# A modulation tile that feeds four column groups, a generator stopped before its last step, and a weight split in two instructions

## The chip, the cores and the metric

The kernel runs on one core of a Trainium2 chip. Its time is the device time of one execution in microseconds (us), the median of the runs taken. Engines are named as in the profile: PE multiplies matrices (PEld is its weight load), DVE, ACT and POOL are the vector, scalar and GpSimd engines, SP issues most of the DMAs. "L577" is line 577 of the kernel.

## The reference

Two layers of a diffusion-style backbone work on 512 latent tokens and 256 context tokens, 1024 wide. Each layer takes six modulation vectors (shift, scale and gate, twice) from a small matrix product of a conditioning vector, normalises and modulates the tokens, mixes them, and runs a gated feed-forward net with a three-tap convolution. The change touches the modulation and the mixer of layer 0:

```python
mod_l = (silu_c @ ada_w[l] + ada_b[l])[:, None, :]        # 1024 x 6144 weights, per layer
mod_c = (silu_cc @ ada_w[l] + ada_b[l])[None, None, :]
sh1, sc1, g1, sh2, sc2, g2 = jnp.split(mod_l, 6, axis=-1)

def even_mixer(hl, hc, w_in, lb, onorm_w, vnorm_w, ws, bs, w_out, with_ctx):
    pl = hl @ w_in                                        # 1024 x 3584 weights
    ...
    al, ac = hgrn2_mixer(...)                             # four heads of a gated linear recurrence
    yl = jnp.concatenate([al, chunk_mlp(...)], -1) @ w_out   # chunk_mlp: gelu(u) * (ws @ norm(gelu(v)))
```

The mixer of layer 1 is a multi-head attention with a Fourier branch beside it; it is not edited, but the modulation of layer 1 is computed while it runs.

## The kernel before, in words

Every large matrix product is done with three fp32r products: a weight and an activation are each split into a high and a low part, and `mm3` (L508 to L510) multiplies high by high, high by low and low by high. A weight chunk is loaded into `raw` by SP (L329), cast to its high part `wh` by ACT (L486), and the low part `wl` is raw minus high, for most chunks one POOL instruction of 128x1024 (L498). A chunk's `raw` comes free for the next load when both have read it.

**Modulation.** `ada_group` computes a third of a layer's modulation. Its weights come in 16 tiles of 128x1024, two for each of eight steps k. The left operand `sc_pad` has only 32 columns (two of them real), so a matmul uses one of four groups of 32 columns of the array and writes 32 partitions of one PSUM bank. A tile makes two matmuls of 512 columns (L577), into the column groups 0 and 1 for an even tile, 2 and 3 for an odd one. Group 1 of layer 0 to group 0 of layer 1 run beside the mixer's input projections (`tick` advances them), the other two groups of layer 1 beside the first steps of the attention: their tiles are loaded into `kt` buffers and later into `ada_t` buffers. The very first part of layer 0's modulation (`first_mods`, L709) already uses all four column groups from one tile, with matmuls of 128 columns.

**Mixer of layer 0.** For each of four heads, four projections (`proj`, L508 to L510) run on PE, and the recurrence of the head before, a generator `gla`, is advanced in steps between them. Its inner steps go round PE (L827, L855), DVE (L848, L868, L870, L872) and ACT (L835). Its end normalises the head's output on DVE (a Newton iteration for the reciprocal root, L460 to L465, then L930), turns it on PE (L939), and splits it (L943, L944). After the last head come the projections `ev_vp` of the gated MLP, whose norm is applied by six POOL instructions (L997), `drain("gla")` (L998), and then four gate projections.

**Order.** The code is written in one order, and a scheduler puts each engine's instructions in another, by its own estimate of when they will be ready; only the first 70 us are placed by hand. So where a line stands in the code doesn't say where it stands on its engine.

Of the kernel before, what the change touches and what calls it, by code (L numbers as in the profile page):

```python
# [16 lines left out]
ALU = mybir.AluOpType  # L17
# [3 lines left out]
P = 128  # L21
D = 1024
KD = D // P
# [263 lines left out]
class _Stream:  # L287
# [112 lines left out]
    def next(self, key):  # L400
        assert self.items[self.pos] == key, (self.items[self.pos], key)
        if self.pos:
            k = self.items[self.pos - 1]
            self.live.pop(k)
            self.own -= set(k[2:])
        while key not in self.hl:
            self.prep()
        while self.ready():
            self.prep()
        self.pos += 1  # L410
        self.load(2 if self.part is None else 3)
        return self.hl.pop(key)
# [3 lines left out]
def backbone(ctx: ExitStack, tc, w, xt, ada, vec, cst, msk, rop, wst, bs, pew, out):  # L416
    nc = tc.nc
    V, S, G, T = nc.vector, nc.scalar, nc.gpsimd, nc.tensor
# [25 lines left out]
    def vcol(name, j=0, n=1):  # L444
        o, wd = VEC[name]
        return vt[:, o + j:o + j + n]

    mods = [cp.tile([P, 48, 2], F32, name=f"mods{l}") for l in range(2)]
# [3 lines left out]
    sc_pad = cp.tile([P, KD, 32], F32, name="sc_pad")  # L452
# [31 lines left out]

    def split(kind, raw, h, l):
        S.copy(h, raw)  # L486
        if kind[:5] == "down1":
            n = raw.shape[-1] // 2
            for e, c in ((G, slice(0, n)), (V, slice(n, 2 * n))):
                e.tensor_tensor(l[:, c], raw[:, c], h[:, c].bitcast(F32), op=ALU.subtract)  # L490
            return
        if kind in by_half:
            for c in range(2):
                c = slice(c * raw.shape[-1] // 2, (c + 1) * raw.shape[-1] // 2)
                G.tensor_tensor(l[:, c], raw[:, c], h[:, c].bitcast(F32), op=ALU.subtract)  # L495
            return
        e = G if kind in on_pool else V
        e.tensor_tensor(l, raw, h.bitcast(F32), op=ALU.subtract)  # L498

    by_half = {"qb_a", "kvb_k", "kvb_v", "od_out"}  # L500
    on_pool = {"dft_c", "ev_v", "qb_a", "qb_b", "kvb_k", "kvb_v", "od_out", "ev_out", "dft_t", "down0_3", "od_f", "od_q", "od_kv", "ev_in", "ev_vp", "up0", "up1"}
# [11 lines left out]
    bg = {"gla": deque(), "ada": deque(), "sum": deque()}  # L513
# [11 lines left out]
    def drain(kind):  # L525
        while advance(kind):
            pass
# [39 lines left out]
    def ada_group(l, g, rest, by=1):  # L567
        base = (l * 3 + g) * 16
        ps = bank("ad")
        for k in range(KD):  # L570
            for hf in range(2):
                i = base + 2 * k + hf
                ada_load(i + 1)
                t = ada_raw.pop(i)
                for j in range(2):
                    q = 2 * hf + j
                    T.matmul(ps[32 * q:32 * q + 32, :], sc_pad[:, k, :], t[:, j * 512:(j + 1) * 512],  # L577
                             start=(k == 0), stop=(k == KD - 1))
            if k % by < by - 1:
                continue  # L580
            ada_load(min(base + 2 * k + 4 + by, 64 if base < 64 else 96))
            for _ in range(rest):
                yield
        asb = tp.tile([P, 512], F32, tag="t2k", name="asb")
        S.copy(asb[:], ps[:])
        yield
        pt = bank("ad")
        for b in range(4):
            T.transpose(pt[:, b * P:(b + 1) * P], asb[:, b * P:(b + 1) * P], ident)
        o = mods[l][:, g * 16:(g + 1) * 16, :].rearrange("p (j b) c -> p b j c", b=4)  # L590
        i0 = pt[:].rearrange("p (b j r) -> p b j r", b=4, r=32)[:, :, :, 0:2]
        i1 = vcol("ada_b", l * 48 + g * 16, 16).rearrange("p (j b) -> p b j", b=4).unsqueeze(3)
        for b in range(4):
            V.tensor_tensor(o[:, b], i0[:, b], i1[:, b].to_broadcast([P, 4, 2]), op=ALU.add)
        yield


# [142 lines left out]
    with tc.manual_schedule(engines={ET.PE, ET.Activation, ET.DVE}):  # L740
# [16 lines left out]
        for s in (1, 0):  # L757
            a, n = SEGS[s]
# [9 lines left out]
        for kk in range(4):  # L768
            wh, wl = ws.next(("ev_v", kk))
            for j in range(2):  # L770
                k = 2 * kk + j
# [23 lines left out]
    def proj(key, src):  # L795

        wh, wl = ws.next(key)
        ps = (bank("mm"), bank("mm"))
        for k in range(KD):
            a = (wh[:, k * P:(k + 1) * P], wl[:, k * P:(k + 1) * P])  # L800
            for s in range(2):
                mm3(ps[s][:, 0:SEGS[s][1]], a, sl(src[k], s), k == 0, k == KD - 1)
            tick()
        return ps

    def gla(h, QG, FF, Y):
        q, sg = QG[:, 0, :], QG[:, 1, :]
# [33 lines left out]
        for lv in range(7):  # L841
# [3 lines left out]
            if lv < 5:  # L845
                dims = [[2 * m, 16 // m], [NT + m, 2], [1, m]]
                ps = blocks(lambda a: pick(QQ, a, dims))
                V.copy_predicated(near[:], mk[:, 32 * lv:32 * lv + 32].unsqueeze(1).to_broadcast([P, 6, 32]), ps)  # L848
            else:
                dims = [[2 * m, P // (2 * m)], [NT + m, 2], [1, m]]  # L850
                for s, (a0, n) in enumerate(SEGS):
                    ps = bank("sc")
# [30 lines left out]
        for g0 in range(0, 10, 4):  # L883
            grp = items[g0:g0 + 4]
            ps = bank("st")
# [5 lines left out]
        for g0 in range(0, 10, 4):  # L891
            grp = items[g0:g0 + 4]
            ps = bank("st")
            for j, (d, i, c) in enumerate(grp):
                T.matmul(ps[:, j * P:(j + 1) * P], KT[:, (g0 + j) * P:(g0 + j + 1) * P], vtile(c, h),
                         start=True, stop=True)
            for j, (d, i, c) in enumerate(grp):
                e = g0 + j
# [10 lines left out]
        for s, (a0, n) in enumerate(SEGS):  # L909
            ps = bank("sc")  # L910
            for j in range(n // P):
                c = a0 // P + j
                o = ps[:, j * P:(j + 1) * P]
                more = [(d, seqs[d].index(c)) for d in range(2) if seqs[d].index(c) > 0]
                T.matmul(o, SC[:, 0, c * P:(c + 1) * P], vtile(c, h), start=True, stop=not more)
                for x, (d, i) in enumerate(more):
                    e = d * 5 + i - 1
                    T.matmul(o, QQ[:, 1 - d, c * P:(c + 1) * P], st[:, e * P:(e + 1) * P],
                             start=False, stop=x == len(more) - 1)
            for j in range(n // P):  # L920
                c = a0 // P + j
# [6 lines left out]
        for s, (a0, n) in enumerate(SEGS):  # L928
# [1 line left out]
            V.tensor_tensor(SC[:, 1, a0:a0 + n].rearrange("p (c t) -> p c t", c=nj),  # L930
                            po[s][:, 0:n].rearrange("p (c t) -> p c t", c=nj),
                            rr[:, a0 // P:a0 // P + nj].unsqueeze(2).to_broadcast([P, nj, P]), op=ALU.mult)
        yield
        Y[h] = xslot()
        for s, (a0, n) in enumerate(SEGS):
            ps = bank("sc")
            for j in range(n // P):
                c = a0 + j * P
# [11 lines left out]
    for h in range(NH_A):  # L950
        QG = xslot(F32)
        FF = xslot(F32)
        for part in (0, 2, 3, 4):
            ps = proj(("ev_in", part * 4 + h), X)
# [40 lines left out]
    for c in range(6):  # L995
        a = vp[c // 3][:, c % 3, :].rearrange("p (g d) -> p g d", g=4)
        G.tensor_tensor(a, a, mr[:, c * 4:c * 4 + 4].unsqueeze(2).to_broadcast([P, 4, P]), op=ALU.mult)  # L997
    drain("gla")  # L998
    for g in range(4):
        ps = proj(("ev_in", 20 + g), X)  # L1000
        U = xcp.tile([P, 2, NT], F32, tag="xc", name="U")
        Y[4 + g] = xslot()
        for s, (a0, n) in enumerate(SEGS):
            u = U[:, 0, a0:a0 + n]
            S.activation(u, ps[s][:, 0:n], AF.Gelu_apprx_tanh)
        for s, (a0, n) in enumerate(SEGS):
            nj = n // P
            p2 = bank("sc")
            for j in range(nj):
                c = a0 // P + j  # L1010
                T.matmul(p2[:, j * P:(j + 1) * P], vp[c // 3][:, c % 3, g * P:(g + 1) * P],
                         wstt[:, g * P:(g + 1) * P], start=True, stop=True)
            z = U[:, 1, a0:a0 + n]
            V.scalar_tensor_tensor(z.rearrange("p (c t) -> p c t", c=nj),
                                   p2[:, 0:n].rearrange("p (c t) -> p c t", c=nj), vcol("vnorm", g),
                                   bsb[:, g * P:(g + 1) * P].unsqueeze(1).to_broadcast([P, nj, P]),
                                   op0=ALU.mult, op1=ALU.add)
            V.tensor_tensor(z, z, U[:, 0, a0:a0 + n], op=ALU.mult)
            yh, yl = sl(Y[4 + g], s)
            S.copy(yh, z)  # L1020
            G.tensor_tensor(yl, z, yh.bitcast(F32), op=ALU.subtract)
# [858 lines left out]
```

## Time and profile before

| | |
|---|---|
| median of 3 runs | 1649.61 us (1648.12 to 1650.98) |
| profiled execution, its own time | 1649.35 us |
| its span, first to last instruction | 1647.6 us |
| PE busy | 1591.9 us (97%) |
| DVE, ACT, POOL busy | 1140.8, 703.4, 649.1 us |
| mean granted clock of PE | 0.992 |

The profile is one execution. In its rows an fp32 matmul shows as two records, so "x4" of L577 are two matmuls. A row of a timeline or of the chain of waits has a start and a length in us; a run of equal instructions is merged into one row with its count. "[0.64 <-DVE qk L868]" behind a row is idle time of the engine just before it, and what ended that.

### The profile page before, as it was taken

The numbers are of one execution on the slowest core, as the hardware profiler recorded it, in microseconds if no ns is written. First come the engines' busy times: TensorE is split into PE (matmuls) and PEld (weight loads), VectorE is DVE, ScalarE is ACT, GpSimd is POOL, SyncE is SP. The second block draws the span as 40 slices with busy tenths as digits, with TensorE's granted clock in tenths as the row PEclk, the third lists the DMA queues.
The fourth block names the chain that finished last, engine by engine and source line by source line (L and its number), as shares of the span: only waits on it lengthen the run. The fifth ranks groups of instructions, "written<-read, shape, count | busy, mean of one in ns | idle before, by whom it ended". The sixth has DMA issues, their size and how long they took to land.

```text
span 1647.6 us, 28314 instructions
## 1 busy us (share of the span) xinstructions
PE 1591.9 (97%) x11206; PEld 1420.5 (86%) x11206; DVE 1140.8 (69%) x2134; ACT 703.4 (43%) x1328; POOL 649.1 (39%) x421
## 2 busy tenths in 40 slices
PE   8999999989999999999999999898899899999998
PEld 7777777678989999999999989676799898999997
DVE  5447675753565666676666775767874799999984
ACT  4323333523444333233332444465665555555551
POOL 1221223344625566565665513331208322323321
PEclk9999999999999999999999999999999999999999
DMA  9453434333412121222212322752105223223222
GB/s 355 159 187 116 142 116 137 120 102 103 130 50 64 61 80 55 74 77 62 80 55 75 90 68 82 250 171 93 52 27 167 90 85 108 103 90 116 103 78 77
DMA packets 53205, 175.11 MB, mean 106 GB/s; under 512 B 5712, under 2 KB 7760, under 8 KB 53072
## 3 DMA queue, kind: packets, MB, share of 16 engines
q1 hardware_dynamic: 51632, 170.66, 31.1%
q10 hardware_dynamic: 1440, 2.64, 0.4%
q8 instruction: 88, 1.44, 0.3%
q14 instruction: 45, 0.37, 0.1%
HBM read 171.18 MB, written 2.10 MB: 105 GB/s over the span
## 4 chain that ended last, share of the span: by engine, by line
PE 79%; DVE 14%; ACT 2%; DMA 2%; issue 2%; POOL 1%; DVEq 0%; SPq 0%; ACTq 0%; POOLq 0%
PE mm L508 17%; PE mm L510 16%; PE mm L509 16%; PE aux L508 7%; PE aux L509 7%; PE aux L510 7%; PE aux L577 2%; DVE qk L870 1%; DVE qk L868 1%; DVE wp L387 1%; PE aux L1143 1%; PE mm L1730 1%; DMA x<-in_xt_dram 1%; DMA raw<-in_w_dram 1%; PE aux L1749 1%
## 5 line engine op out<-in xcount | busy, mean ns | idle before, releaser
L498 POOL TENSOR_TENSOR wl<-raw,wh 128x1024 fp32r<-128x1024 f32 (+5 forms) x100 | 210.2, 2104 | 356.6 <-ACT wh L486 304.5
L486 ACT CAST wh<-raw 128x1024 fp32r<-128x1024 f32 (+5 forms) x155 | 146.5, 947 | 141.0 <-PE mm L509 63.8
L387 POOL TENSOR_TENSOR wp<-sum,wp 128x512 fp32r<-128x512 f32 x80 | 115.9, 1454 | 163.4 <-ACT wp L385 153.9
L508 PE MATMUL mm<-xt,wh 128*128 128x256 f32 (+1 forms) x384 | 135.1, 353 | 0.9 <-ACT xt L648 0.9
L510 PE MATMUL mm<-xt,wl 128*128 128x512 f32 (+1 forms) x384 | 129.4, 338 | 0.0
L509 PE MATMUL mm<-xt,wh 128*128 128x512 f32 (+1 forms) x384 | 129.3, 337 | 0.0
L509 PE MATMUL mm<-slot,wh 128*128 128x512 f32 (+1 forms) x336 | 113.4, 338 | 1.0 <-POOL slot L1253 0.7
L508 PE MATMUL mm<-slot,wh 128*128 128x512 f32 (+1 forms) x336 | 113.5, 339 | 1.0 <-ACT slot L1252 1.0
L510 PE MATMUL mm<-slot,wl 128*128 128x512 f32 (+1 forms) x336 | 113.1, 337 | 0.0
L385 ACT CAST wp<-sum 128x512 fp32r<-128x512 f32 x100 | 60.8, 620 | 122.2 <-PE aux L509 61.5
L1028 DVE SCALAR_TENSOR_TENSOR xl<-mm,mods,xl 128x512 f32<-128x512 f32 (+1 forms) x84 | 58.5, 696 | 70.7 <-PE mm L510 70.2
L495 POOL TENSOR_TENSOR wl<-raw,wh 128x512 fp32r<-128x512 f32 (+2 forms) x50 | 55.7, 1135 | 129.1 <-ACT wh L486 123.6
L387 POOL TENSOR_TENSOR wp<-raw,wp 128x512 fp32r<-128x512 f32 x60 | 80.0, 1341 | 52.3 <-ACT wp L385 52.3
L385 ACT CAST wp<-raw 128x512 fp32r<-128x512 f32 x100 | 62.1, 621 | 78.5 <-DMA raw<-in_w_dram 27.7
L508 PEld LDWEIGHTS mm<-xt,wh 128*128 128x128 f32 x384 | 72.0, 188 | 27.0 <-issue 16.8
L508 PE MATMUL mm<-kt,wp 128*128 128x256 f32 x320 | 90.4, 282 | 3.8 <-ACT t L1216 3.8
L490 POOL TENSOR_TENSOR wl<-raw,wh 128x512 fp32r<-128x512 f32 x22 | 35.7, 1622 | 138.0 <-DVE t L1245 92.3
L510 PE MATMUL mm<-kt,wp 128*128 128x256 f32 x320 | 89.8, 281 | 0.0
L509 PE MATMUL mm<-kt,wp 128*128 128x256 f32 x320 | 89.7, 280 | 0.0
L510 PEld LDWEIGHTS mm<-xt,wl 128*128 128x128 f32 x384 | 72.3, 188 | 8.2
L509 PEld LDWEIGHTS mm<-xt,wh 128*128 128x128 f32 x384 | 72.2, 188 | 8.3
L509 PE MATMUL mm<-lt,wh 128*128 128x256 f32 (+2 forms) x236 | 78.1, 331 | 1.2 <-DVE lt L1253 1.2
(390 smaller groups left out, 5272.7 us busy)
## 6 DMA issues: line engine op xcount, KB each, us to landing
raw<-in_w_dram SPq DMA_DIRECT2D x162, 512.0 KB, 3.5
ada_t<-in_ada_dram SPq DMA_DIRECT2D x80, 512.0 KB, 4.4
raw<-in_w_dram SPq DMA_DIRECT2D x31, 384.0 KB, 3.1
wp<-in_w_dram SPq DMA_DIRECT2D x20, 512.0 KB, 4.4
kt<-in_ada_dram SPq DMA_DIRECT2D x16, 512.0 KB, 7.0
raw<-in_w_dram SPq DMA_DIRECT2D x10, 256.0 KB, 2.6
xl<-in_xt_dram SPq DMA_DIRECT2D x2, 1024.0 KB, 8.0
out_dram<-xl SPq DMA_DIRECT2D x8, 256.0 KB, 2.0
```

What stands on the lines that cost most here:

```text
L385: S.copy(h, a)
L387: e.tensor_tensor(l, a, h.bitcast(F32), op=ALU.subtract)
L486: S.copy(h, raw)
L490: e.tensor_tensor(l[:, c], raw[:, c], h[:, c].bitcast(F32), op=ALU.subtract)
L495: G.tensor_tensor(l[:, c], raw[:, c], h[:, c].bitcast(F32), op=ALU.subtract)
L498: e.tensor_tensor(l, raw, h.bitcast(F32), op=ALU.subtract)
L508: T.matmul(ps, a[0], b[0], start=first, stop=False, **kw)
L509: T.matmul(ps, a[0], b[1], start=False, stop=False, **kw)
L510: T.matmul(ps, a[1], b[0], start=False, stop=last, **kw)
L577: T.matmul(ps[32 * q:32 * q + 32, :], sc_pad[:, k, :], t[:, j * 512:(j + 1) * 512], start=(k == 0), stop=(k == KD - 1))
L868: V.tensor_tensor(qa, qa, pick(FF[:], NT + m, [[2 * m, nb], [-(NT + m), 2], [0, m]]), op=ALU.mult)
L1028: V.scalar_tensor_tensor(xs, ps, gate, xs, op0=ALU.mult, op1=ALU.add)
```

## The change

Three edits. A modulation tile is now used in four matmuls of 256 columns, one for each column group, and the even tile fills the left half of the bank, the odd tile the right half; the bias addition that reads the turned result is re-indexed. The generator `gla` stops before its last step under the name "tail", the mixer runs it that far instead of to its end, and drains it after the first gate projection. And the low part of a mixer weight (`ev_v`, `ev_in`, `ev_vp`, `ev_out`) is computed by two POOL instructions, one for each half of the chunk's columns.

```diff
     def split(kind, raw, h, l):
         S.copy(h, raw)
-        if kind[:5] == "down1":
+        if kind[:5] == "down1" or kind[:3] == "ev_" and kind in on_pool:
             n = raw.shape[-1] // 2
-            for e, c in ((G, slice(0, n)), (V, slice(n, 2 * n))):
+            for e, c in ((G, slice(0, n)), (V if kind[:2] == "do" else G, slice(n, 2 * n))):
                 e.tensor_tensor(l[:, c], raw[:, c], h[:, c].bitcast(F32), op=ALU.subtract)
             return
...
                 t = ada_raw.pop(i)
-                for j in range(2):
-                    q = 2 * hf + j
-                    T.matmul(ps[32 * q:32 * q + 32, :], sc_pad[:, k, :], t[:, j * 512:(j + 1) * 512],
-                             start=(k == 0), stop=(k == KD - 1))
+                for q in range(4):
+                    T.matmul(ps[32 * q:32 * q + 32, hf * 256:(hf + 1) * 256], sc_pad[:, k, :],
+                             t[:, q * 256:(q + 1) * 256], start=k + hf == 0, stop=k + hf == KD, skip_group_check=True)
...
-        yield
+        yield "tail"
         Y[h] = xslot()
...
-    drain("gla")
+    while next(bg["gla"][0]) != "tail":
+        pass
     for g in range(4):
         ps = proj(("ev_in", 20 + g), X)
+        drain("gla")
```

On PE, in the first steps of the attention, this is what stands around the first two `kt` tiles that are used alone. Before (`kt` is a modulation tile, `lt` the latent query, `wh` and `wl` its weight, `mm` and `aux` PSUM banks):

```order
L508 MATMUL mm_10147<-wh_10022,lt_9912 128x384 [waits Activation_49]
L509 MATMUL mm_10147<-wl_10023,lt_9912 128x384 [waits Pool_49]
L577 MATMUL aux_10080<-kt_10089,sc_pad_88 32x512 [waits DMAHW5_49]
L577 MATMUL aux_10080<-kt_10089,sc_pad_88 32x512
L510 MATMUL mm_10147<-wh_10022,lt_9912 128x384 [waits DVE_49]
L508 MATMUL mm_10147<-wh_10135,lt_9913 128x384 [waits Activation_49]
L509 MATMUL mm_10147<-wl_10136,lt_9913 128x384 [waits Pool_49]
L510 MATMUL mm_10147<-wh_10135,lt_9913 128x384 [waits DVE_49]
L577 MATMUL aux_10080<-kt_10091,sc_pad_88 32x512 [waits DMAHW6_49]
L577 MATMUL aux_10080<-kt_10091,sc_pad_88 32x512
```

And after:

```order
L508 MATMUL mm_10307<-wh_10166,lt_10056 128x384 [waits Activation_49]
L576 MATMUL aux_10224<-kt_10241,sc_pad_88 32x256 [waits DMAHW5_49]
L576 MATMUL aux_10224<-kt_10241,sc_pad_88 32x256 x3
L509 MATMUL mm_10307<-wl_10167,lt_10056 128x384 [waits Pool_49]
L510 MATMUL mm_10307<-wh_10166,lt_10056 128x384 [waits DVE_49]
L508 MATMUL mm_10307<-wh_10295,lt_10057 128x384 [waits Activation_49]
L509 MATMUL mm_10307<-wl_10296,lt_10057 128x384 [waits Pool_49]
L510 MATMUL mm_10324<-wh_10166,lt_10055 128x384
L510 MATMUL mm_10307<-wh_10295,lt_10057 128x384 [waits DVE_49]
L576 MATMUL aux_10224<-kt_10243,sc_pad_88 32x256 [waits DMAHW6_49]
L576 MATMUL aux_10224<-kt_10243,sc_pad_88 32x256 x3
```

Each of the two tiles stands alone between the same projections in both programs, one or two matmuls earlier or later; two matmuls of 512 columns have become four of 256.

On PE at the last head's turning (L939), in the first gate projection (`xt` the activations, `scr` the head's output). Before:

```order
L508 MATMUL mm_3465<-xt_550,wh_3319 128x512
L509 MATMUL mm_3465<-xt_550,wh_3319 128x512
L939 MATMUL aux_3445<-ct_74,scr_748 128x128 [waits DVE_49]
L939 MATMUL aux_3445<-ct_74,scr_748 128x128 x3
L939 MATMUL aux_3453<-ct_74,scr_748 128x128 [waits DVE_49,Activation_49]
L939 MATMUL aux_3453<-ct_74,scr_748 128x128
L589 MATMUL aux_3487<-ct_74,asb_3473 128x128 x4
L510 MATMUL mm_3465<-xt_550,wl_3320 128x512
```

And after:

```order
L508 MATMUL mm_3576<-xt_553,wh_3443 128x512
L509 MATMUL mm_3576<-xt_553,wh_3443 128x512
L939 MATMUL aux_3585<-ct_74,scr_753 128x128 [waits DVE_49]
L939 MATMUL aux_3585<-ct_74,scr_753 128x128 x3
L939 MATMUL aux_3593<-ct_74,scr_753 128x128 [waits DVE_49,Activation_49]
L939 MATMUL aux_3593<-ct_74,scr_753 128x128
L588 MATMUL aux_3613<-ct_74,asb_3599 128x128 x4
L510 MATMUL mm_3576<-xt_553,wl_3444 128x512 [waits Pool_49]
```

Nothing moved here but the wait of the last row, which is for the second half of the weight's low part.

## Rows read from the trace of the kernel before

**Rows 1.** The page's table of engines: busy us, share of the span, instructions.

```profile
PE 1591.9 (97%) x11206; PEld 1420.5 (86%) x11206; DVE 1140.8 (69%) x2134; ACT 703.4 (43%) x1328; POOL 649.1 (39%) x421
```

**Rows 2.** The page's chain that ended last: share of the span by engine.

```profile
PE 79%; DVE 14%; ACT 2%; DMA 2%; issue 2%; POOL 1%; DVEq 0%; SPq 0%; ACTq 0%; POOLq 0%
```

**Rows 3.** The timeline of PE where two modulation tiles are used one right behind the other (four matmuls), and the projection behind them.

```profile
70.18 1.06 PE L577 MATMUL aux<-ada_t,sc_pad 128*32 128x512 f32 x8
71.17 0.50 PE L508 MATMUL mm<-xt,wh 128*128 128x512 f32 x1
```

**Rows 4.** The timeline of PE where `first_mods` uses two tiles, sixteen matmuls of 128 columns, four in each column group, and the projection behind them.

```profile
29.18 1.08 PE L709 MATMUL aux<-ada_t,sc_pad 128*32 128x128 f32 x32
30.20 0.50 PE L508 MATMUL aux<-wh,xt 128*128 128x512 f32 x1
```

**Rows 5.** The chain of waits from 1052 to 1076.5 us, in order of time: of its pieces on L577 the first and the last of the six with one tile that come before the one with three tiles (x12), that one, and one more with one tile.

```profile
1053.03 0.98 PE aux L577 x4
...
1067.54 0.98 PE aux L577 x4
1072.92 1.84 PE aux L577 x12
...
1075.24 0.98 PE aux L577 x4
```

**Rows 6.** The timeline of PE where one matmul of a modulation tile stands alone (two records), and what follows.

```profile
208.66 1.05 PE L577 MATMUL aux<-ada_t,sc_pad 128*32 128x512 f32 x2
209.63 0.49 PE L918 MATMUL aux<-qk 128*128 128x128 f32 x2
```

**Rows 7.** The chain of waits from 1086 to 1176 us: pieces on L577 that hold fewer than two whole tiles or are split, and a load on the chain.

```profile
1124.91 1.01 PE aux L577 x4
...
1128.01 3.42 DMA ada_t<-in_ada_dram
...
1131.48 1.05 PE aux L577 x4
...
1134.59 1.43 PE aux L577 x6
...
1136.61 0.98 PE aux L577 x2
```

**Rows 8.** The waits of PE over the whole span: what it waited for, us in total, times, the longest.

```profile
PE aux L827 <- DVE qk L868: 5.2, 4, 1.6
PE aux L939 <- DVE scr L930: 5.2, 2, 5.0
...
PE aux L827 <- ACT scr L835: 2.2, 1, 2.2
...
PE aux L855 <- DVE qk L868: 1.2, 2, 0.6
...
PE mm L510 <- DVE xt L733: 0.6, 1, 0.6
```

**Rows 9.** Groups of POOL instructions by form: busy us, mean ns, idle before.

```profile
L498 POOL TENSOR_TENSOR wl<-raw,wh 128x1024 fp32r<-128x1024 f32 x56 | 135.3, 2416 | 290.2 <-ACT wh L486 273.0 <-PE aux L855 14.3 <-PE aux L827 2.8
...
L944 POOL TENSOR_TENSOR slot<-slot 128x512 fp32r<-128x512 f32 x4 | 5.2, 1296 | 4.4 <-ACT slot L943 4.4
```

**Rows 10.** The timelines of POOL and of DVE in the last head's normalisation.

```profile
337.10 6.03 POOL L997 TENSOR_TENSOR vp<-vp,mr 128x512 f32<-128x512 f32 x6 [2.50 <-DVE mr L465]
...
337.01 0.17 DVE L926 TENSOR_SCALAR ss<-ss 128x6 f32<-128x6 f32 x1
337.21 0.95 DVE L460 TENSOR_SCALAR rr<-ss 128x6 int32<-128x6 int32 x1
...
342.18 0.96 DVE L463 TENSOR_TENSOR rst<-ss,rr 128x6 f32<-128x6 f32 x1
343.18 0.17 DVE L464 SCALAR_TENSOR_TENSOR rst<-rst,rr 128x6 f32<-128x6 f32 x1
```

**Rows 11.** The timelines of POOL and DVE at one low part of a mixer weight, and the same DVE line with POOL idle.

```profile
307.56 2.41 POOL L498 TENSOR_TENSOR wl<-raw,wh 128x1024 fp32r<-128x1024 f32 x1 [7.40 <-ACT wh L486]
...
307.66 3.12 DVE L868 TENSOR_TENSOR qk<-qk,slot 128x768 f32<-128x768 f32 x1
...
314.71 0.95 DVE L868 TENSOR_TENSOR qk<-qk,slot 128x768 f32<-128x768 f32 x1
```

**Rows 12.** The timelines of POOL and DVE at two low parts, one right behind the other.

```profile
59.64 5.22 POOL L498 TENSOR_TENSOR wl<-raw,wh 128x1024 fp32r<-128x1024 f32 x2 [7.93 <-ACT wh L486]
...
59.33 3.29 DVE L729 SCALAR_TENSOR_TENSOR mt<-x,w,rall 128x256 f32<-128x256 f32 x2
62.55 3.26 DVE L733 SCALAR_TENSOR_TENSOR xt<-mt,mods,xt 128x256 fp32r<-128x256 f32 x2
```

**Rows 13.** Busy us (and instructions) of PE, PEld, DVE, ACT and POOL in three stretches, with the clock that PE was granted, the DMAs' share and GB/s.

```profile
340.00:344.28 4.28, 0.00 (x0) 0.00 (x0) 3.97 (x10) 0.00 (x0) 3.12 (x4) 1.00 0.76 283
344.28:347.69 3.41, 2.77 (x12) 2.67 (x13) 2.39 (x8) 0.83 (x2) 0.13 (x1) 0.50 0.00 1
1080.00:1190.00 110.00, 98.19 (x638) 78.75 (x636) 90.87 (x274) 67.03 (x169) 26.94 (x26) 0.98 0.30 104
```

More of the change, by code (lines that the diff above doesn't have):

```diff
@@ L589, in ada_group @@
             T.transpose(pt[:, b * P:(b + 1) * P], asb[:, b * P:(b + 1) * P], ident)
-        o = mods[l][:, g * 16:(g + 1) * 16, :].rearrange("p (j b) c -> p b j c", b=4)
+        o = mods[l][:, g * 16:(g + 1) * 16, :].rearrange("p (f j e) c -> p f e j c", f=2, e=2)
         i0 = pt[:].rearrange("p (b j r) -> p b j r", b=4, r=32)[:, :, :, 0:2]
-        i1 = vcol("ada_b", l * 48 + g * 16, 16).rearrange("p (j b) -> p b j", b=4).unsqueeze(3)
+        i1 = vcol("ada_b", l * 48 + g * 16, 16).rearrange("p (f j e) -> p f e j", f=2, e=2).unsqueeze(4)
         for b in range(4):
-            V.tensor_tensor(o[:, b], i0[:, b], i1[:, b].to_broadcast([P, 4, 2]), op=ALU.add)
+            f, e = divmod(b, 2)
+            V.tensor_tensor(o[:, f, e], i0[:, b], i1[:, f, e].to_broadcast([P, 4, 2]), op=ALU.add)
         yield
```

## The prediction

> **What bounds the kernel now.** I read the engine table first, then the chain that ended last, then the waits of PE, and only then the timelines of the places that the diff touches. PE is busy for 97% of the span [rows 1] and holds 79% of the chain, DVE 14% [rows 2]. So PE work taken away counts where it lies on the chain, and a DVE or POOL instruction counts where a wait of PE ends on it; the waits of PE are few, and the ones that this change can reach are listed in [rows 8]. No wait of PE ends on a weight's high or low part (`wh`, `wl`), so the weights themselves are early everywhere. The sum is made against the profiled execution, 1649.35 us, 0.26 below the median of the three runs.
>
> **Edit 1: a tile feeds four column groups.** In layer 0 the two tiles of a step mostly stand right behind each other, and PE already runs their four matmuls beside each other in four column groups: from their start to the next matmul 0.99 us pass [rows 3]. A tile that stands alone has two matmuls in two groups, and takes 0.98 us on the chain [rows 5]: half the work in the same time, since each group still streams 2 records of 512 columns. What counts is the columns that the fullest group streams: 1024 in both cases; 2048 where three tiles stand together, 1.84 us [rows 5]. That gives (1.84 - 0.98) / 1024 = 0.84 ns a column and 0.12 us around it.
>
> With the change one tile puts 2 records of 256 columns into each group: 512 columns, so 0.12 + 0.43 = 0.55, and 0.43 us less. I take 0.41, since `first_mods` shows four groups fed from one tile with many short records: eight records of 128 columns in each group, again 1024 columns, take 1.02 us where two of 512 take 0.99 [rows 4, 3], so six more records cost 0.03. That row is also the proof that four groups can read one tile at once.
>
> - Attention's first steps, 1052 to 1076 us: seven tiles alone and one group of three lie on the chain [rows 5], and the order keeps all eight where they were. Gain 7 x 0.41 + 0.43 = 3.3 us. PE is what holds this stretch up; the tiles come in about as they are used, so part may turn into waiting for a load. Lower bound half of it, 1.6.
> - Later attention, 1086 to 1176: two tiles alone, 1.01 and 1.05, and a knot of 1.43 + 0.98 [rows 7], which becomes 1 + 7 + 1 matmuls, about 0.55 + 1.00 + 0.55. That would be 0.41 + 0.41 + 0.31 = 1.1 us, but a load of 3.42 us stands on the chain ahead of the second [rows 7], and in 1080 to 1190 DVE is busy for 91 and PE for 98 of 110 us [rows 13], each waiting for the other. I take 0.4, bounds 0 and 1.1.
> - Layer 0: one matmul of a tile alone costs 0.97 us [rows 6] and becomes 0.55: 0.4. A second one of this kind ends in a wait for DVE, so nothing. Bounds 0 and 0.8.
> - About 30 places where the tiles stand in pairs get two more records in each group, 0.01 us each: 0.3 us slower.
>
> The Trainium skill speaks against this edit: "TensorEngine Tiling (Array Packing)", Instruction Overhead, gives each matmul about 60 cycles, whatever its size. By that page the 160 further matmuls, 320 records, at 25 ns (60 cycles of the 2.4 GHz clock, an estimate) would cost 8 us and eat the whole gain. The trace disagrees here: 24 more records than in a pair of tiles cost 0.03 us [rows 3, 4], since those of different groups start beside each other.
>
> **Edit 2: the last head's output is turned later.** PE waits 5.0 us for L930 ahead of L939 [rows 8], and the half-rate clock of the 3.41 us behind it (0.50 granted [rows 13]) costs 1.7 more. But the order of PE shows L939 on the same place in both programs, behind the same matmul of the first gate projection, and DVE's order around L930 is the same too: the scheduler had already laid the projection over the drain. So nothing is saved. What causes this wait stays: six POOL instructions L997 run for 6.03 us from 337.10, and in that time each small DVE instruction takes 0.95 where it takes 0.17 before and behind [rows 10].
>
> **Edit 3: the low part in two halves.** One low part takes POOL 2.42 us [rows 9]; for a half I take the 128x512 subtraction of L944, 1.30 us [rows 9]. Two make 2.6, so 48 chunks cost POOL 48 x 0.15 = 7 us more; it is busy 39% [rows 1], and PE never waits for `wl`, so that and the earlier first half are worth nothing. SP's loads of `raw` wait for POOL and come 0.15 later; two of them also stand behind a pair of modulation loads that they stood ahead of. The weights are early enough for both.
>
> What does count is DVE. L868 takes 0.95 us with POOL idle and 3.12 when it starts just behind a low part [rows 11]: it stands until POOL's instruction ends, as L460 to L463 stand behind L997 [rows 10]. And where POOL has a next instruction ready, the waiting DVE instruction still gets in between: in [rows 10] one per POOL instruction, and in [rows 12] two low parts take 5.22 us, not 2 x 2.42, since a DVE instruction held the second up. So with halves a standing instruction is let in after 1.30 us instead of 2.42, and gains 1.1. If a second one of the kind follows, it stands behind the second half: 1.30 + 1.30 + about 0.4 of holding up + 0.8 = 3.8 us, against 2.42 + 0.8 + 0.95 = 4.2 before. So 1.1 us where one instruction matters, 0.35 where two do.
>
> The waits of PE that end on such a DVE instruction: L827 and L855 on L868 (5.2 and 1.2), on L835, which follows L870 (2.2), and L510 on L733 (0.6) [rows 8]. Eight waits, 9.2 us. L733's 0.6 goes whole. Of the L855 waits the first, 0.6, is [rows 11], with nothing behind it: whole. Of the others I count four at 0.35, two at nothing: 1.4. Together 2.6 us. Bounds: 1.1 for each as far as the wait is that long, 6.7; and, if the second half is let in ahead of DVE each time, 8 x 0.15 = 1.2 slower. At the tail a small DVE instruction ahead of L997 stands 0.15 longer: 0.15 slower.
>
> The Trainium skill has this as a rule ("SBUF — State Buffer", Who interferes with whom): a DVE instruction with two SBUF inputs and a GpSimd one that reads SBUF exclude each other, and the one that was issued first has it for its whole length. The trace agrees: 3.12 against 0.95 [rows 11]. By that rule two halves are two holds, which is what the 0.35 and 1.1 above rest on.
>
> **The sum.** -3.3 - 0.4 - 0.4 + 0.3 - 2.6 + 0.15 = -6.25 us: 1643.1 for the profiled execution, 1643.3 against the median. All bounds on the good side: -3.3 - 1.1 - 0.8 + 0.3 - 6.7 = -11.6, 1638; all on the bad side: -1.6 + 0.3 + 1.2 + 0.15 = +0.05, 1649.7.
>
> **The rivals.**
>
> - A, the tiles' gain is swallowed: loads or DVE set the pace of the attention's first steps, and PE waits where it worked. For it: the load on the chain in [rows 7], and DVE's 91 of 110 us in [rows 13]. Against it: seven of the eight groups of [rows 5] are chain pieces with PE work before and behind. Then 2.6 + 0.4 - 0.45 = 2.5 remain: 1647.1.
> - B, the halves give nothing: POOL's second half is let in ahead of the waiting DVE instruction. Against it stand [rows 10, 12]. Then -4.1 + 0.3 + 1.2 + 0.15: 1647.1.
> - C, slower: the modulation's matmuls have new lengths, and the scheduler has put the attention's steps between 1080 and 1190 us in another order on PE, DVE and ACT. PE is idle there for 110 - 98.19 = 11.8 us [rows 13]. If that order makes a reduction or a turn late, waits grow; it decides once they grow by more than the 6.25 gained. At double the idle time: 1649.6 - 6.25 + 11.8 = 1655.2. For it: no rule makes the new order better or worse; against it: its moves are by a few places each, and none crosses a projection.
> - D, edit 2 works after all, because DVE reaches L930 earlier: 5.0 + 1.7 us more, 1636.6. Against it: the unchanged order and L997.
> - E, four groups cannot read one tile side by side and run in turn: a tile takes 4 x 0.43 + 0.12 = 1.84 us, so each of 30 pairs 3.6 for 1.0 and each of 9 lone tiles 1.84 for 0.98, 78 + 8 us in all: near 1735. Against it: [rows 4].
>
> **How the numbers follow.** Forecast (edits 1 and 3 as priced, the new order neutral within 2 us) 0.60; A 0.13; B 0.11; C 0.09; D 0.05; E 0.02. A difference of 0.2%, 3.3 us, is about what a measurement of this kernel can tell from none. The forecast lies under 1646.3 with nine parts in ten, and D with it: faster 0.54 + 0.05, and a third of A and B, where the bounds give more than the price: 0.67. Slower: C, E, and a little of the bad bounds: 0.11. The rest, 0.22, is no change. The range is 1637 to 1650: it holds the bounds of the unknown costs and A and B, and leaves out E, most of C and the better half of D.
>
> **What would show it.** Right: L577's successor has one-tile pieces of 0.55 to 0.6 us on the chain in the attention's first steps, and pairs at 1.00; L939 still waits about 5 us for L930; the two halves of a low part take 1.3 us each, with the DVE instruction between them and L868 at 2 us at most; the waits L827, L855 and L510 sum to some 6.5 instead of 9.2 us. Wrong: one-tile pieces near 1 us or more, new waits of PE on loads behind them, L868 still at 3 us, or waits in 1080 to 1190 well over 12 us.

## The result and the profile after

| | before | after |
|---|---|---|
| median us (runs) | 1650.30 (4) | 1639.85 (4) |
| ratio of times, 95% interval | | 0.9938 [0.9915, 0.9961] |
| profiled execution, its own time | 1649.35 | 1638.32 |
| its span | 1647.6 | 1636.5 |

The change is faster by 10.4 us, with an interval of 6.4 to 14. A later comparison of the same two kernels gave 0.9949 [0.9934, 0.9964], 8.6 us; the two edits that do something gave 3.3 us each when they ran alone. The time stands inside the range, the forecast of 1643.3 on the cautious side. Two single slow executions (6011.80 us of edit 2 alone, 1760.83 us of the kernel held back and in quarters) are left out of every figure here.

The page's tables of engines and of the chain's shares, as in [rows 1, 2]:

```profile
PE 1582.2 (97%) x11526; PEld 1428.8 (87%) x11526; DVE 1136.5 (69%) x2134; ACT 704.1 (43%) x1328; POOL 668.4 (41%) x469
...
PE 80%; DVE 14%; ACT 2%; DMA 2%; issue 1%; POOL 1%; DVEq 0%; ACTq 0%; SPq 0%; POOLq 0%
```

PE has 320 more records and is busy for 9.7 us less; POOL is busy for 19.3 us more, not the 7 of the prediction: a POOL instruction that waits its turn behind DVE counts as busy (3.27 us for a pair against 2.51, below). These rows alone don't say what PE's 9.7 us are made of.

The chain of waits in the attention's first steps, the pieces on L576 (L577 before), to set beside [rows 5]:

```profile
1048.79 0.57 PE aux L576 x8
...
1050.60 0.57 PE aux L576 x8
...
1057.74 1.00 PE aux L576 x16
...
1066.11 1.43 PE aux L576 x24
...
1067.91 0.57 PE aux L576 x8
```

A tile alone: 0.57 where it took 0.98. Two together: 1.00, as before. Three: 1.43, where they took 1.84. The steps are 0.43 us each, the price that the prediction took from [rows 5].

The waits of PE over the whole span, to set beside [rows 8]:

```profile
PE aux L939 <- DVE scr L930: 5.3, 2, 5.1
PE aux L827 <- DVE qk L868: 4.7, 5, 1.6
...
PE mm L508 <- ACT pr L1740: 3.3, 3, 1.9
...
PE aux L827 <- ACT scr L835: 2.2, 1, 2.2
...
PE mm L508 <- ACT lt L1349: 1.8, 2, 1.5
```

The waits of L855 on L868 (1.2) and of L510 on L733 (0.6) are gone, L827 on L868 fell by 0.5: together 6.9 us where there were 9.2. L939 still waits. The row of L1349 is larger than before (0.8); its cause follows with the third experiment. The wait for L1740, the exponential of the attention's softmax, was 1.3 in before (L1738 there); it comes with edit 1's new order (3.5 with edit 1 alone, 1.3 with edit 3 alone), and the part on the prediction takes it up. The stretch where it stands, to set beside the last of [rows 13]:

```profile
1073.00:1183.00 110.00, 98.54 (x709) 82.58 (x710) 88.84 (x277) 67.00 (x168) 25.63 (x26) 0.97 0.29 105
```

The timelines of POOL and of DVE at the low part that stood in [rows 11]:

```profile
302.47 3.27 POOL L490 TENSOR_TENSOR wl<-raw,wh 128x512 fp32r<-128x512 f32 x2 [5.92 <-ACT wh L486]
306.52 3.50 POOL L490 TENSOR_TENSOR wl<-raw,wh 128x512 fp32r<-128x512 f32 x2 [0.78 <-ACT wh L486]
...
302.94 1.65 DVE L868 TENSOR_TENSOR qk<-qk,slot 128x768 f32<-128x768 f32 x1
...
305.11 0.74 DVE L872 TENSOR_TENSOR slot<-slot 128x48 f32<-128x48 f32 x1
...
306.93 1.95 DVE L868 TENSOR_TENSOR qk<-qk,slot 128x768 f32<-128x768 f32 x1
...
312.01 0.95 DVE L868 TENSOR_TENSOR qk<-qk,slot 128x768 f32<-128x768 f32 x1
```

The L868 that took 3.12 us [rows 11] takes 1.65. It got in behind the first half, and that held the second half up: the two take 3.27 us, while a pair that meets no DVE instruction takes 2.51 (first row of the timelines of the normalisation, below). From it to the next L868 3.99 us pass; in [rows 11] it was 314.71 - 307.66 = 7.05. The next low part comes a step earlier for that, beside the second L868, which takes 1.95 for 0.95, and its step 5.08 us. L872 behind the first L868 takes 0.74; in before it stood beside a second low part:

```profile
311.26 2.37 POOL L498 TENSOR_TENSOR wl<-raw,wh 128x1024 fp32r<-128x1024 f32 x1 [1.29 <-ACT wh L486]
...
311.30 2.43 DVE L872 TENSOR_TENSOR slot<-slot 128x48 f32<-128x48 f32 x1
```

The timelines of POOL, DVE and PE in the last head's normalisation, to set beside [rows 10]:

```profile
325.86 2.51 POOL L490 TENSOR_TENSOR wl<-raw,wh 128x512 fp32r<-128x512 f32 x2 [3.68 <-ACT wh L486]
330.87 6.03 POOL L997 TENSOR_TENSOR vp<-vp,mr 128x512 f32<-128x512 f32 x6 [2.50 <-DVE ss L926]
...
330.91 1.03 DVE L460 TENSOR_SCALAR rr<-ss 128x6 int32<-128x6 int32 x1
...
335.96 0.97 DVE L463 TENSOR_TENSOR rst<-ss,rr 128x6 f32<-128x6 f32 x1
336.96 0.17 DVE L464 SCALAR_TENSOR_TENSOR rst<-rst,rr 128x6 f32<-128x6 f32 x1
...
338.71 1.54 PE L939 MATMUL aux<-ct,scr 128*128 128x128 f32 x6 [5.12 <-DVE scr L930]
```

Nothing here is different from before: six DVE instructions of 1 us beside six POOL instructions, then 0.17 us each, and PE waits 5.12 us.

**Where the lead arises.** The next table is worked out from the traces: the start of the same PE instruction in before minus that in the other kernel, at six times of before's trace. Columns: the changed kernel, its second profile, edit 1 alone, edit 3 alone, and edit 2 alone, whose instructions are those of before.

| at (us of before) | after | again | edit 1 | edit 3 | edit 2 |
|---|---|---|---|---|---|
| 62 | 2.3 | 2.1 | 1.6 | 2.4 | 0.7 |
| 325 | 6.4 | 4.7 | -1.6 | 4.8 | -0.7 |
| 600 | 4.0 | 0.6 | -5.0 | 0.3 | -2.3 |
| 1040 | 5.3 | 1.9 | -3.6 | 1.7 | -0.9 |
| 1080 | 7.6 | 5.2 | -1.4 | 1.6 | -1.3 |
| 1640 | 11.0 | 6.5 | 0.0 | 0.1 | -2.7 |

The column of edit 2 is the noise: two executions of one order of instructions drift apart by up to 3.4 us there, and the two of the changed kernel by 4.5. So one trace settles the places, and only the repeated times settle the total.

The lead of 2 us at 62 us shows how such a drift arises: it is the clock's. The same 6.83 us in before and then in the changed kernel, busy us of PE, PEld, DVE, ACT and POOL, and the granted clock behind them:

```profile
16.60:23.43 6.83, 6.36 (x69) 5.38 (x58) 1.97 (x13) 1.12 (x3) 2.28 (x1) 0.50 1.03 407
```

```profile
16.60:23.43 6.83, 5.41 (x109) 4.41 (x101) 4.53 (x18) 2.47 (x6) 2.50 (x2) 1.00 1.03 407
```

The kernel with edits 1 and 3, whose order is that of the changed kernel, was at half rate for 6.83 us there too, and its lead at 62 us is 0.6. So nothing shows that these 2 us, of the first profile's 11, belong to an edit.

### The profile page after: what moved, and what is told of

Its sections match the earlier page's. It is cut to its first block, busy times and chain, and to the rows that moved or that the text cites. A ratio compares the mean times of both kernels' runs of the same rounds, so it can differ in the third digit from the quotient of the medians.

```text
span 1636.5 us, 29026 instructions
## 1 busy us (share of the span) xinstructions
PE 1582.2 (97%) x11526; PEld 1428.8 (87%) x11526; DVE 1136.5 (69%) x2134; ACT 704.1 (43%) x1328; POOL 668.4 (41%) x469
## 4 chain that ended last, share of the span: by engine, by line
PE 80%; DVE 14%; ACT 2%; DMA 2%; issue 1%; POOL 1%; DVEq 0%; ACTq 0%; SPq 0%; POOLq 0%
PE mm L508 17%; PE mm L510 17%; PE mm L509 17%; PE aux L508 7%; PE aux L509 7%; PE aux L510 7%; PE aux L576 2%; DVE qk L870 1%; DVE wp L387 1%; DMA ada_t<-in_ada_dram 1%; DVE qk L868 1%; PE aux L1145 1%; PE mm L1732 1%; PE aux L1751 1%; PE aux L855 1%
## 5 line engine op out<-in xcount | busy, mean ns | idle before, releaser
L490 POOL TENSOR_TENSOR wl<-raw,wh 128x512 fp32r<-128x512 f32 x118 | 170.5, 1462 | 371.0 <-ACT wh L486 222.3
L498 POOL TENSOR_TENSOR wl<-raw,wh 128x768 fp32r<-128x768 f32 (+6 forms) x52 | 94.3, 1815 | 102.8 <-ACT wh L486 46.0
L510 PE MATMUL mm<-xt,wl 128*128 128x512 f32 (+1 forms) x384 | 130.4, 340 | 0.0
L510 PE MATMUL mm<-slot,wl 128*128 128x512 f32 (+1 forms) x336 | 112.4, 335 | 0.0
L510 PE MATMUL mm<-kt,wp 128*128 128x256 f32 x320 | 89.8, 281 | 0.0
L510 PEld LDWEIGHTS mm<-xt,wl 128*128 128x128 f32 x384 | 73.2, 191 | 8.2
```

Of the source, the lines that this page charges most:

```text
L510: T.matmul(ps, a[1], b[0], start=False, stop=last, **kw)
```

## The experiments

**Edit 1 alone.**

```diff
-                for j in range(2):
-                    q = 2 * hf + j
-                    T.matmul(ps[32 * q:32 * q + 32, :], sc_pad[:, k, :], t[:, j * 512:(j + 1) * 512],
+                for q in range(4):
+                    T.matmul(ps[32 * q:32 * q + 32, hf * 256:(hf + 1) * 256], sc_pad[:, k, :],
+                             t[:, q * 256:(q + 1) * 256],
```

> Edit 1 alone (four matmuls of 256 columns per modulation tile; the other two edits undone). Theory A, the edits add up as priced: a lone tile takes 0.57 us where it took 0.98, but in the attention's first steps part of the 3.3 us turns into waits for ACT and DVE (in the trace of the change that stretch gave 2.3 us, from 5.3 to 7.6 ahead), so 2.5 to 4 us faster than before, ratio 0.9976 to 0.9985, and nothing gained ahead of 1040 us but some 0.4 in layer 0. Rival B, most of the 10 us is edit 1's, since the attention's new order also takes waits away there: 6 to 8 us faster, ratio 0.9952 to 0.9964.

Measured: 0.998 [0.997, 0.999], 3.3 us faster, as theory A has it. The waits that edit 3 is to reach stay as they were:

```profile
PE aux L827 <- DVE qk L868: 5.5, 4, 1.9
...
PE aux L855 <- DVE qk L868: 1.2, 2, 0.6
```

Between 1040 and 1080 us of the table it gains 2.3 us (2.27 before rounding), as the changed kernel does; in the changed kernel's second profile that stretch gives 3.3. What differs between those is told behind the third experiment.

**Edit 3 alone.**

```diff
-        if kind[:5] == "down1":
+        if kind[:5] == "down1" or kind[:3] == "ev_" and kind in on_pool:
...
-            for e, c in ((G, slice(0, n)), (V, slice(n, 2 * n))):
+            for e, c in ((G, slice(0, n)), (V if kind[:2] == "do" else G, slice(n, 2 * n))):
```

> Edit 3 alone (each low part of a mixer weight in two POOL instructions; on PE, DVE, ACT and SP the order is that of before, only POOL's differs). Theory A, DVE is let in between the halves: L868 never stands for 3 us, the waits L827 and L855 on L868, L827 on L835 and L510 on L733 fall from 9.2 to about 6.9 us in all as in the trace of the change; 2.5 to 4 us faster, ratio 0.9976 to 0.9985. Rival B, the halves give nothing of their own and the gains seen at those places in one trace belong to that execution: those waits sum to over 8.5 us, and the time is within 1 us of before. The L939 wait for L930 stays at about 5 us under both.

Measured: 0.998 [0.9971, 0.9989], 3.3 us faster, as theory A has it. Its waits of PE:

```profile
PE aux L939 <- DVE scr L930: 5.3, 2, 5.1
PE aux L827 <- DVE qk L868: 4.3, 5, 1.3
...
PE aux L827 <- ACT scr L835: 2.2, 1, 2.2
```

6.5 us of the 9.2, L855 on L868 and L510 on L733 gone, L939's wait as it was.

**Edits 1 and 3 without edit 2.**

```diff
-        yield "tail"
+        yield
...
-    while next(bg["gla"][0]) != "tail":
-        pass
+    drain("gla")
```

> Edits 1 and 3 without edit 2. On every engine its instructions stand in the same order as in the changed kernel. Theory A, edit 2 does nothing: the time of the changed kernel, ratio to before 0.9938 within 0.0025, and the sum of the gains of the two edits alone within 2 us. Rival B, edit 2 is worth something after all: 3 us or more slower than the changed kernel, ratio 0.996 or more.

Measured: 0.9954 [0.9939, 0.9968], 7.3 us faster, by median 2.8 us slower than the changed kernel's first four runs and the same as its later five (1642.66 and 1642.68). The sum of the two edits alone is 6.6. This is theory A.

These profiles also show what made the stretch behind 1040 us worth 2.3 or 3.3 us. Four DVE instructions L1452 stand there beside two low parts of small weights on POOL. In the changed kernel's first profile, DVE and POOL:

```profile
1040.24 3.16 DVE L1452 TENSOR_SCALAR qt<-qt,rsd 128x384 f32<-128x384 f32 x4
...
1040.42 2.43 POOL L498 TENSOR_TENSOR wl<-raw,wh 128x384 fp32r<-128x384 f32 x2 [0.72 <-DMA raw<-in_w_dram]
```

and in its second:

```profile
1043.69 2.14 DVE L1452 TENSOR_SCALAR qt<-qt,rsd 128x384 f32<-128x384 f32 x4
...
1043.87 1.08 POOL L498 TENSOR_TENSOR wl<-raw,wh 128x384 fp32r<-128x384 f32 x1 [0.72 <-ACT wh L486]
1045.65 1.32 POOL L498 TENSOR_TENSOR wl<-raw,wh 128x516 fp32r<-128x516 f32 x1 [0.69 <-ACT wh L486]
```

Where the second low part follows the first within 0.5 us, the four L1452 take 1 us more, ACT turns `lt` out later, and PE waits 1.4 to 1.9 us for it; where there is a pause of 0.7, PE waits 0.3 to 0.8. All twelve profiles of this study fall into these two kinds, and the same program into either. The clock goes with it: in the five of the first kind PE was at half rate for 3.4 us there, in six of the seven of the second kind for 6.8.

**The norm on ACT.** Twenty-four ACT instructions in place of the six L997:

```diff
-        G.tensor_tensor(a, a, mr[:, c * 4:c * 4 + 4].unsqueeze(2).to_broadcast([P, 4, P]), op=ALU.mult)
+        for j in range(4):
+            S.activation(a[:, j], a[:, j], AF.Copy, scale=mr[:, c * 4 + j:c * 4 + j + 1])
```

> The changed kernel with the norm of the gated MLP's values (L997, six POOL instructions with two inputs) done by 24 ACT instructions of 128x128 with a scale per partition instead. Theory A, L939 waits for L930 because the small DVE instructions ahead of L930 stand behind those POOL instructions: now they take 0.17 us each, L930 ends about 4.7 us earlier, the wait of 5.1 us goes, and with it part of the half-rate clock behind it (1.7 to 3.4 us of work at half rate gives 0.8 to 1.7): 5 to 7 us faster than the changed kernel, ratio to before 0.9895 to 0.991. Rival B, the wait is due to what comes ahead of that chain on DVE or to ACT, and moves elsewhere: the same as the changed kernel within 1.5 us.

Measured: 0.9948 [0.9934, 0.9963], 1641.5 us, 1.2 under the kernel without edit 2 beside it. The outcome of B, for a reason that the timelines of ACT, DVE and PE show:

```profile
333.22 7.14 ACT L998 ACTIVATE vp<-vp,mr 128x128 f32<-128x128 f32 x24 [0.98 <-DVE mr L465]
340.26 0.25 ACT L923 ACTIVATE junk<-aux 128x128 f32<-128x128 f32 x1
...
341.15 0.17 DVE L926 TENSOR_SCALAR ss<-ss 128x6 f32<-128x6 f32 x1 [7.96 <-ACT junk L923]
...
346.31 1.54 PE L939 MATMUL aux<-ct,scr 128*128 128x128 f32 x6 [3.17 <-DVE scr L930]
```

The scheduler put the new instructions ahead of the last three squares L923 that the chain starts from. So the chain began 8 us late, and then ran at 0.17 us an instruction until a low part came by. The wait had only changed its maker; about POOL this decided nothing, and the next one was built to.

**The same POOL instructions, held back.** One DVE instruction gives `mr` back unchanged (mr plus 0 times the last head's reciprocal root `rr`, which `gla` now hands out), and L997 reads that:

```diff
+    V.scalar_tensor_tensor(mr[:], last_rr[0][:, 0:1].to_broadcast([P, 24]), 0.0, mr[:],
+                           op0=ALU.mult, op1=ALU.add)
     for c in range(6):
         a = vp[c // 3][:, c % 3, :].rearrange("p (g d) -> p g d", g=4)
```

> The changed kernel with one more DVE instruction (its result is mr itself: mr plus 0 times the last head's reciprocal root), which makes the six POOL instructions on vp wait until the last head's normalisation is done; on all engines the order is otherwise that of the changed kernel. Theory A, the wait of L939 is made by these POOL instructions alone: the small DVE instructions take 0.17 us all the way, L930 ends 4.5 to 5 us earlier, the wait falls from 5.1 to under 0.6 us and little half-rate clock follows it: 4.5 to 6 us faster than the changed kernel as run beside it. Rival B, the POOL instructions moved back hold up what comes behind them (the low parts and the turned output, or the matmuls on vp some 24 places behind L939): a new wait of 3 us or more there, less than 2 us gained.

Measured: 0.991 [0.9891, 0.9928], 1634.58 us, 8.1 under the changed kernel beside it. This is theory A, with more gained than expected. DVE, POOL and PE there (line numbers a few higher than in the changed kernel):

```profile
334.32 0.17 DVE L463 TENSOR_TENSOR rst<-ss,rr 128x6 f32<-128x6 f32 x1
334.52 0.17 DVE L464 SCALAR_TENSOR_TENSOR rst<-rst,rr 128x6 f32<-128x6 f32 x1
...
336.11 6.04 POOL L1002 TENSOR_TENSOR vp<-vp,mr 128x512 f32<-128x512 f32 x6 [5.94 <-DVE mr L999]
...
335.67 0.88 PE L940 MATMUL aux<-ct,scr 128*128 128x128 f32 x6 [0.28 <-DVE scr L930]
...
342.20 0.94 PE L1016 MATMUL aux<-wstt,vp 128*128 128x128 f32 x6 [0.51 <-POOL vp L1002]
```

The POOL instructions take the same 6.04 us, only later; no small DVE instruction of the chain takes over 0.2, and the wait is 0.28 instead of 5.1. B's new wait exists, and is 0.5. The same 16.5 us of both profiles, busy us of PE, PEld, DVE, ACT and POOL, and the granted clock behind them; held back:

```profile
333.50:350.00 16.50, 15.63 (x96) 13.33 (x95) 7.40 (x21) 3.76 (x7) 13.04 (x12) 1.00 0.41 145
```

and the changed kernel beside it:

```profile
333.50:350.00 16.50, 11.38 (x63) 10.04 (x62) 11.16 (x23) 2.73 (x5) 8.18 (x9) 0.79 0.31 115
```

Without the idle 5 us PE was granted full speed throughout, and did 96 instructions instead of 63. The half-rate stretch behind the wait, and one at 460 us, in the changed kernel beside it:

```profile
337.56:344.39 6.83, 4.00 (x16) 3.81 (x17) 5.48 (x16) 0.92 (x2) 2.39 (x4) 0.50 0.12 43
...
460.50:467.33 6.83, 5.98 (x25) 5.63 (x25) 6.33 (x16) 3.38 (x8) 0.00 (x0) 0.50 0.00 0
```

PE had work for only 4.00 of the first 6.83 us, so that half rate costs some 2 us; the rest of it lies inside the wait. By the starts of the same PE instructions in these two traces, the wait gives 4.8 us, the clock behind it 1.9, and 1.1 are lost again where the matmuls on `vp` stand: 5.6 us in all from this place. Another 2.9 us come at 460 us, where the held-back kernel has no half-rate stretch. No edit lies there; the changed kernel's first profile has 3.41 us at half rate at that place, and whether the hold does away with the stretch or it is scatter isn't shown.

**The low part in quarters.**

```diff
+        if kind[:3] == "ev_" and kind in on_pool:
+            n = raw.shape[-1] // 4
+            for c in range(4):
+                c = slice(c * n, (c + 1) * n)
+                G.tensor_tensor(l[:, c], raw[:, c], h[:, c].bitcast(F32), op=ALU.subtract)
+            return
```

> The changed kernel with each low part of a mixer weight in four POOL instructions of 256 columns. Theory A, a standing DVE instruction is let in at the next border: L868 takes at most 1.5 us (1.95 with halves, 3.12 with one piece), the waits L827 on L868 and L835 fall by another 0.5 to 1.5 us from 6.9, PE's order is the same, 0 to 2 us faster than the changed kernel. Rival B, each piece is a hold of its own and a chain of DVE instructions pays at every border: those waits stay at 6.5 us or more and the time is the same or up to 2 us slower.

Measured: 0.9933 [0.9918, 0.9948], 3.3 us under the changed kernel beside it by the medians; the intervals overlap. The direction is theory A's, with more gained than it expected, in time and in the waits (L833 is L827 here, L874 and L841 are L868 and L835):

```profile
PE aux L833 <- DVE qk L874: 2.1, 4, 0.7
...
PE aux L833 <- ACT scr L841: 1.2, 1, 1.2
```

3.3 us where halves left 6.9 and whole parts 9.2. One figure missed: the longest L868 is 2.17 us, not under 1.5.

**Four short matmuls in two groups.** The kernel before, each matmul of a tile cut in two:

```diff
-                    T.matmul(ps[32 * q:32 * q + 32, :], sc_pad[:, k, :], t[:, j * 512:(j + 1) * 512],
-                             start=(k == 0), stop=(k == KD - 1))
+                    for c in range(2):
+                        T.matmul(ps[32 * q:32 * q + 32, c * 256:(c + 1) * 256], sc_pad[:, k, :],
+                                 t[:, j * 512 + c * 256:j * 512 + (c + 1) * 256],
+                                 start=k + c == 0, stop=k + c == KD, skip_group_check=True)
```

> The kernel before with each matmul of a modulation tile cut in two of 256 columns in the same column group (four matmuls per tile as in edit 1, but two groups instead of four). Theory A, what counts is the columns that the fullest group streams: a lone tile still takes 0.98 to 1.05 us on the chain of the attention's first steps, and the time is that of before, from 1 us faster to 2 us slower. Rival B, the shorter matmuls or the new order give the gain of edit 1: a lone tile at 0.6 us, or 3 us faster than before all the same.

Measured: 1.000 [0.9989, 1.0011], as theory A has it. Its chain in the attention's first steps:

```profile
1053.52 0.99 PE aux L578 x8
...
1055.41 0.99 PE aux L578 x8
...
1064.16 1.02 PE aux L578 x16
```

A tile alone with eight records in two groups: 0.99. In four groups, eight records of the same length: 0.57. The number and the length of the matmuls do nothing by themselves.

**The changed kernel again**, beside the three above, without an edit.

> The changed kernel once more, beside the others. Theory A, the true effect is the sum of the two edits alone (3.3 and 3.3 us) and the ratio to before is 0.9945 to 0.996; the 10 us of the first comparison were partly the scatter of single executions. Rival B, it is 0.994 or less.

Measured: 0.9949 [0.9934, 0.9964]. This is theory A by its value; the interval of the first comparison overlaps it.

**Held back and in quarters together**, the edits of those two experiments in one kernel.

> The changed kernel with the POOL instructions on vp held back until the last head's normalisation is done, and with the low parts in quarters: the two that gained, together. Theory A, they act at different places (330 to 340 us, and the steps of the recurrence ahead of that) and add: 8 + 3 us faster than the changed kernel, ratio to before 0.987 to 0.990, the waits L827 on L868 2.1 us and L940 on L930 under 0.6. Rival B, part of each gain was the same scatter of the half-rate clock: ratio 0.9905 to 0.992.

Measured: 0.9886 [0.9871, 0.9901], 1630.85 us by the median of three. This is theory A: 19.3 us faster than before, and by the ratios some 10 faster than the change.

**Edit 2 alone**, the reverse of the diff of the third experiment, on the kernel before.

> Edit 2 alone. Its instructions stand in the order of before on every engine, so both theories give the time of before, ratio 0.9985 to 1.0015; what it shows beside that is how far two runs of the same instructions lie apart.

Measured: 0.9995 [0.9985, 1.0004]. As expected; the scatter it shows is the last column of the table above.

## Why the prediction was right

- **Edit 1, first steps of attention: -3.3.** The price of a tile, 0.55, was 0.57. From the first lone tile to 1080 us the lead grows by 3.6 to 3.7 us in all four profiles with edits 1 or 1 and 3, and not at all in those of edit 2 and edit 3 alone: the 3.3 of the sum was right, and nothing of it turned into waiting for a load. What makes 2.3 or 3.3 us of it between 1040 and 1080 us lies ahead of the first tile: the wait for ACT and the half rate told behind the third experiment.
- **Edit 1, later attention: -0.4.** Not to be read: the kernels without edit 1 drift by more than that there. The new order brought the longer wait for L1740, the longest 1.9 us, but the idle time of PE that rival C looked to did not grow: 11.5 us in the changed kernel where it was 11.8 [rows 13]. That the new order costs 6 us or more (rival C) is excluded by the run of edit 1 alone, that four groups run in turn (E) by the 0.57.
- **Edit 1, layer 0: -0.4, and the pairs +0.3.** The single matmul that took 0.97 us [rows 6] is two records of 256 columns now, with 0.55 to the next matmul; a pair takes 1.00 for 0.99. Together with the attention the run gave 3.3 us where the sum was 3.8.
- **Edit 2: nothing.** So it was, in the repeated times too. Its 5 us had the maker that the prediction named: only moving L997 took them away.
- **Edit 3: -2.6 + 0.15.** The run gave 3.3. The tail's 0.15 is there (5.1 for 5.0 [rows 8]). By the leads of the four profiles with edit 3, L733's wait, priced at 0.6, gave 0.9. The waits of L827, most of the "four at 0.35", gave less than priced: on L868 and L835 together 7.4 us before, 6.9 in the changed kernel and 6.5 with edit 3 alone. The term that was too small is the two waits of L855, priced at 0.6 and at most 0.35: they gave 1.6. The prediction read the first of them, [rows 11], as having "nothing behind it", but a second low part stood there, and L872 beside that: 2.43 us, and 0.74 in the changed kernel. So the step of [rows 11] gained 3.1 us (7.05 to 3.99); the step behind it gave part of that back, and 1.6 us of lead remain of the two. The rule of the prediction held, and its count of what stood where did not: that the sum of edit 3 came out near is partly luck, since terms missed on both sides. And 0.6 us, which no term held, came between 76 and 112 us, where PE waits for nothing: its matmuls follow each other a few ns closer in each profile with halves. What causes that wasn't tried.
- **The sum**, -6.25, stands beside 6.6 for the edits alone, 7.3 without edit 2, and 8.6 and 10.4 for the changed kernel. (Its 1643.3 against the median is 1643.36.) No step is behind the last 2 to 4 us. In the two profiles of the first comparison, 11 us of span apart, 2 us lie ahead of 62 us, in the clock. The first profile and the second differ by 4.5 us of span at a mean granted clock of 0.993 and 0.989: 0.004 of 1640 us, twice over, is about 13 us at half rate, which can cost at most half of that, 6.6. So the clock's stretches, which the prediction left as they were in before, are enough to make the difference between runs of one program. Whether the change also makes them rarer is open.
- **Rivals A, B and D** are out: edit 1 alone and edit 3 alone gave 3.3 us each, edit 2 none.

## What to carry to other kernels

Some DVE instructions that stand beside a longer POOL instruction are priced by that instruction's length and not by their own, here those of the recurrence and of the normalisation (0.17 or 0.95 us became 1 to 3). Not all are: the two that read the turned output from PSUM (L941 of the held-back kernel) took 1.14 us beside a POOL instruction, as the changed kernel's L940 did with POOL idle. So look for small DVE instructions of 1 us where 0.2 is usual, and then either cut the POOL instruction or, worth far more where its result isn't needed soon, make it wait until the chain on DVE is through (8.1 us here, against 3.3 for the cut). An edit of the code's order is worth what the scheduled order shows, and one that moves no instruction is worth nothing. With narrow left operands, count the columns of the fullest column group, not the matmuls.

## What the runs showed that was not expected

The instructions held back were expected to give 4.5 to 6 us and gave 8.1: in the traces 5.6 of it come from the place of the old wait, the rest from half-rate stretches elsewhere, whose cause is open. A TENSOR_SCALAR of 128x384 with one SBUF operand and a column of scalars stood beside POOL as well, 3.16 us for 2.14 in a group of four. And one program's two profiles can differ by 4.5 us of 1640 with no instruction in another place.
